# Forgetting and query columns as pairs among the mixer's first products, their sums kept in PSUM, the recurrence projected first

## The chip, the cores and the metric

The kernel runs on one core of a Trainium2 chip. The time is device time in microseconds (us) of one execution of the whole block, from the first instruction to the last. Work is spread over the core's engines: TensorE (PE in the profile, its weight loads PEld), VectorE (DVE), ScalarE (ACT), GpSimd (POOL) and SyncE (SP), which here only issues transfers. Each engine runs its own list of instructions in a fixed order and waits at semaphores for what the others produce.

## What is computed

One layer of a decoder for 1024 positions of 1024 channels: a half-step SwiGLU feed-forward part (called ffn1 below), a token mixer, a second feed-forward part (ffn2), a last norm. Every matrix product is of 1024 x 1024 activations with a weight. The mixer, cut to what matters:

```python
q, f, i, og, u, ga, gb = jnp.split(h @ w_in, IN_SPLITS, axis=-1)
q = silu(q) * DK ** -0.5
fg = lb + (1.0 - lb) * jax.nn.sigmoid(f)          # forgetting
o = hgrn2_chunked(q, 1 - fg, i, log(fg))          # 8 heads, gated linear recurrence
o = o * lax.rsqrt(mean(o * o) + EPS) * hgrn_g * silu(og)
y_a = o @ hgrn_w_o
ua, ub = jnp.split(u, 2, axis=-1)
u = causal_depthwise_conv(ua * sigmoid(ub), conv_w, conv_b)    # 31 taps
y_b = silu(layer_norm(u, conv_ln_g, conv_ln_b)) @ conv_w_o
return (sigmoid(ga) * y_a + sigmoid(gb) * y_b) @ w_out
```

q, f, i, og, ga and gb are 8 columns of 128 channels each, u is 16.

## The kernel before

Activations lie with channels on the 128 partitions and positions along the row, in two halves of 512 positions. Every fp32 matrix product is made of three fp32r products, high x high, high x low and low x high; `split` makes the two parts, the high one with a cast on ACT (L90) and the low one with a subtraction on DVE (L91). One matrix instruction multiplies a 128x128 weight tile with a 128x512 operand and adds into one PSUM bank. A column (128 outputs, 8 weight tiles, two halves) made directly takes 8 x 2 x 3 = 48 of them (`mm3`, L104 to L106), a pair of columns 96.

`paired` makes a pair of columns with seven products instead of eight quarter products, each of 4 x 3 = 12 instructions (`mmw`, L232 to L234), so 84 in all. For that it needs sums of quarter operands. The right operands' sums (x11, x12, x21, x22 of the activations, 16 for a stage) are subtractions on POOL, L290, once per stage; their splits are the tiles `hq`, `bq` and some of `h`. The weights' sums (four for a pair, L251 and L306) and splits (seven) are on DVE and ACT, in `prepare`, one pair ahead. The products' sums (seven for a pair, L323 to L335) are on DVE and read PSUM; one copy out of PSUM, L321, is on ACT. The first two pairs of a stage are made directly (`warm`), while the norm of the stage before ends. `paired` runs three times: in ffn1, in the mixer and in ffn2.

The stages in order, with the stretch of the trace: ffn1 (0 to 697 us); the mixer's first products (697 to 1017), 16 pairs, namely 8 of u's columns (i and 8 + i, for the convolution) and 8 of the two gates' columns; the units (1017 to 1585); the merge (1585 to about 1850); ffn2. There are 8 units, one for each head of the recurrence. A unit makes four columns directly: forgetting, query, i and og, 192 instructions; then `head` makes the recurrence: six levels of decayed scores (L563, L579 on PE, then on DVE qa L583, k L584 and a masked copy out of PSUM L590), the states st (L618, L627), a norm (`on` L643 to L649, a reciprocal root of small DVE operations, L174 to L179), transposes on PE (L653) and the output og (L655). The depthwise convolution of one column (`conv`) is 1 + 30 DVE operations over 1024 positions (L541, L543); two of the eight (CONV_EARLY) run beside the mixer's first products, six in the units. At the end of the units stands the convolution's projection of the first half (`convolved(0)`). The merge projects the recurrence of each half, then mixes.

A scheduler lays the instructions out: it goes by priorities, which follow the order in which the code is written; a convolution is put back by `conv_delay`, so that its operations fill what DVE has free. Each engine then runs its list in that fixed order. POOL also holds some low splits of the warm pairs (L91 on POOL).

Of the kernel before, what the change touches and what calls it, by code (L numbers as in the profile page):

```python
# [8 lines left out]
F32 = mybir.dt.float32  # L9
# [19 lines left out]
CONV_EARLY = (1, 4)  # L29
# [11 lines left out]
class Block:  # L41
# [187 lines left out]
    def mmw(self, ps, w, i, x, first, last):  # L229
        wh, wl = w[:, 0, i * P:(i + 1) * P], w[:, 1, i * P:(i + 1) * P]  # L230
        mm = self.nc.tensor.matmul
        mm(ps, wh, x[:, 0, :], start=first, stop=False)  # L232
        mm(ps, wh, x[:, 1, :], start=False, stop=False)  # L233
        mm(ps, wl, x[:, 0, :], start=False, stop=last)  # L234
# [7 lines left out]
    def paired(self, ctx, h, hctx, src, order, warm, emit, after, right, ready=()):  # L242
# [17 lines left out]
        self.part(ctx, wp=11, hq=8, bq=4)  # L260
# [24 lines left out]
        b11, b21, b22 = ([b1[hh, k0 + i] for i in range(4)] for hh, k0 in ((0, 0), (0, 4), (1, 4)))  # L285
        t1, t2, t3, t4 = [], [], [], []
        for i in range(4):
            x11, x12, x21, x22 = h[0][i], h[1][i], h[0][4 + i], h[1][4 + i]
            for o, x, y in ((x11, x12, x11), (x12, x22, x12), (x22, x22, x11), (x21, x21, x22)):
                nc.gpsimd.tensor_tensor(o, x, y, op=sub)  # L290
            t2.append(hq(x22))
            t3.append(hq(x12))
            t1.append(self.parts(x11))
            t4.append(self.parts(x21, self.bq, "bq"))
        hctx.close()
        self.part(ctx, right=True, **right)

        def product(ps, w, xs):
            for i in range(4):
                self.mmw(ps, w, i, xs[i], i == 0, i == 3)  # L300

        def prepare(f):
            ra, rb = load(f)
            a11, a12, a21, a22 = ra[:, :T], ra[:, T:], rb[:, :T], rb[:, T:]
            w11, w12, w22 = wop(a11), wop(a12), wop(a22)
            V.tensor_tensor(a22, a21, a22, op=add)  # L306
            tt(a21, a11, a21)
            tt(a11, a22, a11)
            tt(a12, a12, a11)
            ws2, ws3, ws1, ws4 = wop(a11), wop(a21), wop(a22), wop(a12)  # L310
            return w11, w12, w22, ws1, ws2, ws3, ws4

        ops = None
        for n, f in enumerate(order):
            if f not in fs:
                w11, w12, w22, ws1, ws2, ws3, ws4 = ops if ops else prepare(f)
                ops = prepare(order[n + 1]) if n + 1 < len(order) else None
                p1, p2, p3, p4, p5, p6, p7 = [self.acc() if (7 * n + i) % 2 == 0 else self.bank() for i in range(7)]
                product(p1, w11, b11)
                c11, c21, c22, u = (self.piece() for _ in range(4))  # L320
                A.copy(u, p1)  # L321
                product(p2, w12, b21)
                V.tensor_tensor(c11, p2, u, op=add)  # L323
                product(p3, ws2, t2)
                V.tensor_tensor(u, p3, u, op=add)
                product(p4, ws3, t3)
                V.tensor_tensor(c22, p4, u, op=add)
                product(p5, w22, t4)
                V.tensor_tensor(c21, p5, c22, op=add)
                emit(f, 0, c11, c21, c21)  # L330
                product(p6, ws1, t1)
                V.tensor_tensor(c22, p6, c22, op=add)
                V.tensor_tensor(u, p6, u, op=add)
                product(p7, ws4, b22)
                V.tensor_tensor(u, p7, u, op=add)  # L335
                emit(f, 1, u, c22, c22)
            after(n, f)
# [6 lines left out]
    def ffn(self, h, hctx, w_in, w_out, gate, warm, residual, norm, done, between=None):  # L344
# [6 lines left out]
        gs = {f: [] for f in order}  # L351
# [4 lines left out]
        def swiglu(f, hh, a, b, dst):  # L356
            s = self.half()
            if dst is None:
                dst = self.half()
            A.activation(s, a, AF.Silu)  # L360
            V.tensor_tensor(dst, b, s, op=ALU.mult)
            gs[f].append(dst)

        def combos(i):

            (x11, x12), (x21, x22) = gs[i], gs[NKK + i]
# [135 lines left out]
    def role(self, tag, shape=(P, S), bufs=2):  # L502
        pool = self.up if tag in ("u", "fg", "k", "q", "og", "v") else self.vp
# [11 lines left out]
    def unit(self, c, hs):  # L515
# [14 lines left out]
        for i, evac in ((8, ev_f), (0, self.silu_into(q)), (16, ev_i), (24, self.silu_into(og))):  # L530
            self.column(hs, self.weight(w_in[i + c]), evac)
# [21 lines left out]
    def head(self, c, fg, k, v, q, og):  # L553
# [96 lines left out]
        for b in range(2):  # L650
# [4 lines left out]
            V.scalar_tensor_tensor(og[:, sl], ps, self.col(C_HG, c), og[:, sl], op0=ALU.mult, op1=ALU.mult)  # L655
            nc.sync.dma_start(self.o_dram[b][c], og[:, sl])
# [20 lines left out]
    def run(self):  # L677
# [4 lines left out]
        self.o_dram = [[self.dp.tile([P, T], F32, name=f"od{h}{i}") for i in range(8)] for h in range(2)]  # L682
# [3 lines left out]
        self.u_dram = [[self.dp.tile([P, T], F32, name=f"ad{h}{i}") for i in range(8)] for h in range(2)]  # L686
        self.z_dram = [[self.dp.tile([P, T], F32, name=f"zd{h}{i}") for i in range(8)] for h in range(2)]
# [103 lines left out]
        def mix_in(f, hh, x, y, dst):  # L791
            sx = x if dst is not None else self.half()
            A.activation(sx, x, AF.Sigmoid)
            if f >= NH:
                sy = y if dst is not None else self.half()
# [3 lines left out]
            elif f in CONV_EARLY:  # L799
                if hh == 0:  # L800
# [11 lines left out]
        with ExitStack() as ctx:  # L812
            w_mix = lambda f, b: a["mix_w_in"][(40 - 8 * b + f) if f < NH else (48 + 8 * b + f - NH)]
            b1 = self.paired(ctx, xs, hctx, w_mix, [f for i in range(NH) for f in (i, NH + i)], warm, mix_in, after,
                             dict(cq=8, up=1, vp=1), ready)
# [3 lines left out]
        late = [c for c in range(NH) if c not in CONV_EARLY]  # L819
        with ExitStack() as ctx:  # L820
            self.part(ctx, wp=8, mp=1, up=2, vp=2, ln=8)
# [16 lines left out]
            for c in range(NH):  # L838
                if c < len(late):
                    u = self.role("u", bufs=1)  # L840
                    for h in range(2):
                        nc.sync.dma_start(u[:, h * T:(h + 1) * T], self.u_dram[h][late[c]])
                    self.conv(late[c], u)
                if c == NH - 1:
                    xc = self.layer_norm(0)
                self.unit(c, h2)
            self.convolved(0, xc)
# [3 lines left out]
        with ExitStack() as inner:  # L851
            self.part(inner, wp=8, gt=4, ol=8, ln=8, nq=3)
# [62 lines left out]
    def merge(self):
# [106 lines left out]
```

## Time and profile before

| | us |
|---|---|
| median of 3 runs | 2467.28 |
| lowest and highest | 2462.15, 2468.10 |
| the profiled execution, its own time | 2467.12 |
| its span in the trace | 2465.3 |
| PE busy in it | 2405.5 |
| DVE busy in it | 2010.2 |
| ACT busy in it | 944.8 |
| POOL busy in it | 116.9 |

The span is what the trace covers; the time has some 1.8 us around it. Busy time is the union of an engine's instructions; those of an engine overlap a little (the next one starts before the last one's end is drawn), so the distance from start to start of two like instructions is what one costs, and less than the duration given for it.

### The profile page before, as it was taken

Reading aid. Unit: us, or ns where it says so; the run is one execution under the profiler, and the core shown is the slowest. Engines: PE = TensorE matmul, PEld = TensorE weight load, DVE = VectorE, ACT = ScalarE, POOL = GpSimd, SP = SyncE. Lnnn points to the kernel's source line nnn. Section 1 sums busy time; section 2 is a strip of 40 time slices with the busy share of each in tenths; the row PEclk is TensorE's granted clock in tenths of the full one; section 3 lists DMA queues with packets and bytes.
Section 4 is the critical chain, followed back from the end, with each engine's and each line's share of the span. In section 5 each row is a group of like instructions: output and inputs, shape, how many; then the busy total and the mean of one; then the engine's idle time right before and its main releaser. Section 6 shows DMA issues by size and latency. Waiting matters only on the chain.

```text
span 2465.3 us, 30875 instructions
## 1 busy us (share of the span) xinstructions
PE 2405.5 (98%) x11320; PEld 1992.7 (81%) x11320; DVE 2010.2 (82%) x3010; ACT 944.8 (38%) x1679; POOL 116.9 (5%) x77
## 2 busy tenths in 40 slices
PE   4999999999999999999999999999999999999997
PEld 3788887888878888788888888888888888888886
DVE  8999999778889999799999877575568777775977
ACT  4522223344644333233333335453343333324443
POOL 3300000000050000000000000000050000000000
PEclk9999999999999999999999999999999999999998
DMA  7156665595523323311212112774523233228743
GB/s 277 68 190 208 202 203 186 174 344 176 171 86 116 106 83 104 105 52 65 68 44 65 56 56 90 241 251 162 159 80 124 86 107 117 93 86 298 269 128 124
DMA packets 139975, 346.46 MB, mean 141 GB/s; under 512 B 15536, under 2 KB 15664, under 8 KB 139824
## 3 DMA queue, kind: packets, MB, share of 16 engines
q1 hardware_dynamic: 139680, 343.97, 41.7%
q8 instruction: 89, 1.46, 0.2%
q10 hardware_dynamic: 144, 0.52, 0.1%
q14 instruction: 62, 0.51, 0.1%
HBM read 266.31 MB, written 78.12 MB: 140 GB/s over the span
## 4 chain that ended last, share of the span: by engine, by line
PE 80%; DVE 12%; DMA 5%; issue 2%; ACT 1%; POOL 0%; SPq 0%; DVEq 0%; ACTq 0%
PE pa L233 8%; PE pa L234 8%; PE pa L232 8%; PE pb L232 8%; PE pb L234 8%; PE pb L233 8%; PE pa L106 8%; PE pa L104 8%; PE pa L105 8%; PE pb L579 3%; DMA ada<-in_ada_w_dram 2%; DVE w L91 2%; DMA ra<-in_ffn_w_in_dram 1%; DVE ada L154 1%; DVE ra L251 1%
## 5 line engine op out<-in xcount | busy, mean ns | idle before, releaser
L90 ACT CAST w<-ra 128x512 fp32r<-128x512 f32 x402 | 238.4, 619 | 436.5 <-DMA ra<-in_ffn_w_in_dram 110.8
L104 PE MATMUL pa<-h,wh 128*128 128x512 f32 x896 | 355.4, 397 | 1.5 <-ACT wh L90 1.5
L106 PE MATMUL pa<-h,wl 128*128 128x512 f32 x896 | 353.7, 395 | 1.8 <-DVE wl L91 1.8
L105 PE MATMUL pa<-h,wh 128*128 128x512 f32 x896 | 353.3, 394 | 0.0
L543 DVE SCALAR_TENSOR_TENSOR uc<-u,par,uc 128x1023 f32<-128x1023 f32 (+14 forms) x240 | 303.1, 1263 | 2.7
L91 DVE TENSOR_TENSOR w<-ra,w 128x512 fp32r<-128x512 f32 x378 | 254.8, 690 | 10.0 <-ACT w L90 9.4
L232 PE MATMUL pa<-h,w 128*128 128x512 f32 x504 | 199.3, 398 | 5.8 <-ACT h L90 4.1
L233 PE MATMUL pa<-h,w 128*128 128x512 f32 x504 | 199.7, 396 | 2.9 <-DVE h L91 2.9
L234 PE MATMUL pb<-h,w 128*128 128x512 f32 x504 | 197.4, 392 | 4.1 <-POOL w L91 4.0
L234 PE MATMUL pa<-h,w 128*128 128x512 f32 x504 | 198.1, 393 | 0.0
L106 PEld LDWEIGHTS pa<-h,wl 128*128 128x128 f32 x896 | 168.6, 188 | 36.0 <-DVE wl L91 2.5
L104 PEld LDWEIGHTS pa<-h,wh 128*128 128x128 f32 x896 | 168.8, 188 | 35.3 <-ACT wh L90 2.3
L233 PE MATMUL pb<-h,w 128*128 128x512 f32 x504 | 197.0, 391 | 0.0
L232 PE MATMUL pb<-h,w 128*128 128x512 f32 x504 | 196.7, 391 | 0.0
L105 PEld LDWEIGHTS pa<-h,wh 128*128 128x128 f32 x896 | 168.9, 189 | 33.2 <-issue 0.7
L90 ACT CAST ob<-br 128x512 fp32r<-128x512 f32 x154 | 95.8, 622 | 198.6 <-PE pb L234 80.1
L90 ACT CAST wh<-raw 128x1024 fp32r<-128x1024 f32 x80 | 84.0, 1051 | 205.5 <-PE pa L105 192.6
L91 DVE TENSOR_TENSOR ob<-br,ob 128x512 fp32r<-128x512 f32 x154 | 106.7, 694 | 67.5 <-ACT ob L90 66.8
L233 PE MATMUL pa<-ob,oa 128*128 128x512 f32 x352 | 137.5, 391 | 1.5 <-DVE ob L91 1.5
L232 PE MATMUL pa<-ob,oa 128*128 128x512 f32 x352 | 137.1, 390 | 0.0
L234 PE MATMUL pa<-ob,oa 128*128 128x512 f32 x352 | 137.0, 389 | 0.0
L360 ACT ACTIVATE s<-c 128x512 f32<-128x512 f32 x80 | 50.6, 633 | 185.4 <-DVE c L335 127.6
(233 smaller groups left out, 5015.6 us busy)
## 6 DMA issues: line engine op xcount, KB each, us to landing
ra<-in_ffn_w_in_dram SPq DMA_DIRECT2D x88, 512.0 KB, 4.2
br<-bd SPq DMA_DIRECT2D x154, 256.0 KB, 3.2
bd<-c SPq DMA_DIRECT2D x146, 256.0 KB, 2.0
ada<-in_ada_w_dram SPq DMA_DIRECT2D x72, 512.0 KB, 4.4
ar<-in_ffn_w_out_dram SPq DMA_DIRECT2D x88, 256.0 KB, 4.5
ra<-in_mix_w_in_dram SPq DMA_DIRECT2D x32, 512.0 KB, 3.8
raw<-in_mix_w_in_dram SPq DMA_DIRECT2D x32, 512.0 KB, 3.5
ar<-in_ffn_w_out_dram SPq DMA_DIRECT2D x22, 512.0 KB, 4.8
```

The lines of the kernel that those rows point to most:

```text
L90: self.nc.scalar.copy(hi, src)
L91: (eng or self.nc.vector).tensor_tensor(lo, src, hi.bitcast(F32), op=ALU.subtract)
L104: mm(ps, wh, x[:, 0, :], start=first, stop=False)
L105: mm(ps, wh, x[:, 1, :], start=False, stop=False)
L106: mm(ps, wl, x[:, 0, :], start=False, stop=last)
L154: self.nc.vector.scalar_tensor_tensor(raw, raw, 1.0, self.cs, op0=ALU.mult, op1=ALU.mult, accum_out=dst)
L232: mm(ps, wh, x[:, 0, :], start=first, stop=False)
L233: mm(ps, wh, x[:, 1, :], start=False, stop=False)
L234: mm(ps, wl, x[:, 0, :], start=False, stop=last)
L360: A.activation(s, a, AF.Silu)
L543: V.scalar_tensor_tensor(uc[:, j:], u[:, :S - j], cw(KC - 1 - j), uc[:, j:], op0=ALU.mult, op1=ALU.add)
L579: mm(ps[0:n, i * 64:(i + 1) * 64], ch(k, i)[:, 0:n], two(ch(qa, i))[:, :, 1, :], start=True, stop=True)
```

## The change

- Forgetting and query columns, eight pairs, go from the units into the mixer's `paired`. Two of the eight gate pairs (GATES_LATE) go out of it and become direct columns at the end of the units. The mixer's `paired` then has 22 pairs, two of them warm. The results are stored to memory (f_dram, q_dram) and loaded by the unit, where Sigmoid and Silu read them from there.
- In the mixer's `paired` (`inbank=True`) sums of products are made by PE in PSUM: `chain` takes w11 b11, is copied by ACT (p1), goes on with ws2 t2, is copied (u2), goes on with ws3 t3 and at last w22 t4; `low` takes ws1 t1, is copied (p6), goes on with ws4 b22. DVE keeps three sums for a pair (seven before), ACT has three copies (one before). The last two products of a pair run among the next pair's.
- The right operands' sums of all three `paired` go from POOL to DVE, with the first `prepare` ahead of them.
- Four convolutions run early, four in the units, at every second one.
- o of the first half stays on chip; the recurrence of both halves is projected first in the merge, with the layer norm of the first half inside it, and `convolved(0)` follows there.

```diff
-CONV_EARLY = (1, 4)
+CONV_EARLY = (1, 2, 4, 5)
+GATES_LATE = (6, 7)
...
+    def sooner(self, n):
+        return self.defer(-n)
...
-        self.part(ctx, wp=11, hq=8, bq=4)
+        self.part(ctx, wp=9 if inbank else 11, **({"w22": 2} if inbank else {}), hq=8, bq=4)
...
-        for i in range(4):
-            x11, x12, x21, x22 = h[0][i], h[1][i], h[0][4 + i], h[1][4 + i]
-            for o, x, y in ((x11, x12, x11), (x12, x22, x12), (x22, x22, x11), (x21, x21, x22)):
-                nc.gpsimd.tensor_tensor(o, x, y, op=sub)
...
+        ops = prepare(order[2])
...
+        for x11, x12, x21, x22 in xx:
+            tt(x11, x12, x11)
+        if inbank:
+            part1()
+        for x11, x12, x21, x22 in xx:
+            tt(x12, x22, x12)
+            tt(x22, x22, x11)
+            t2.append(hq(x22))
+            t3.append(hq(x12))
+        for x11, x12, x21, x22 in xx:
+            tt(x21, x21, x22)
+            t4.append(self.parts(x21, self.bq, "bq"))
...
+        def up(dst, src):
+            with self.sooner(200):
+                A.copy(dst, src)
+        def third(chain, ws3, t3, p6, c12, c22, f):
+            product(chain, ws3, t3, True)
+            with self.sooner(200):
+                V.tensor_tensor(c22, chain, p6, op=add)
+            emit(f, 1, c12, c22, c22)
+        def fourth(chain, w22, c11, n, f):
+            product(chain, w22, t4, True)
+            emit(f, 0, c11, chain, c11)
+            after(n, f)
...
+            product(chain, w11, b11)
+            up(p1, chain)
+            if not old:
+                second()
+            if old:
+                third(*old[0])
+            product(low, ws1, t1)
+            up(p6, low)
+            if old and not last:
+                second()
+            product(chain, ws2, t2, True)
+            up(u2, chain)
+            if old:
+                fourth(*old[1])
+            product(low, ws4, b22, True)
+            V.tensor_tensor(c12, low, u2, op=add)
...
-        for i, evac in ((8, ev_f), (0, self.silu_into(q)), (16, ev_i), (24, self.silu_into(og))):
+        for h in range(2):
+            sl = slice(h * T, (h + 1) * T)
+            nc.sync.dma_start(fg[:, sl], self.f_dram[h][c])
+            nc.sync.dma_start(q[:, sl], self.q_dram[h][c])
+        for h in range(2):
+            sl = slice(h * T, (h + 1) * T)
+            ev_f(fg[:, sl], h, sl)
+            A.activation(q[:, sl], q[:, sl], AF.Silu)
+        for i, evac in ((16, ev_i), (24, self.silu_into(og))):
...
-                if c < len(late):
-                    u = self.role("u", bufs=1)
+                if c % 2 == 0:
+                    u = self.role("u")
...
-            self.convolved(0, xc)
+            for c in GATES_LATE:
+                for b in range(2):
...
+                    self.column(h2, self.weight(a["mix_w_in"][48 + 8 * b + c]), ev_g)
```

How the lists of instructions change. First PE in the fourth unit, from the transposes that end its head (L653 before, L754 after). In the names, `pa` and `pb` are PSUM banks, `wh` and `wl` the high and low parts of a column's weight, `on` the normed recurrence, `q` and `k` the next head's. Before, the transposes, with columns (L104 to L106) behind them:

```order
L106 MATMUL pa_12014<-h_5439,wl_12011 128x512
L653 MATMUL pb_11841<-par,on_11798 128x128 x2
L104 MATMUL pa_12014<-h_5442,wh_12010 128x512
L653 MATMUL pb_11848<-par,on_11798 128x128 x2
L892 MATMUL pb_11855<-usum,mean 128x512
L653 MATMUL pb_11848<-par,on_11798 128x128 x2
L105 MATMUL pa_12014<-h_5442,wh_12010 128x512
```

After, where L110 to L112 are the columns, L664 and L680 the next head's scores:

```order
L754 MATMUL pb_11121<-par,on_11078 128x128 x2
L111 MATMUL pa_11627<-h_6216,wh_11597 128x512
L754 MATMUL pb_11128<-par,on_11078 128x128
L664 MATMUL pb_11268<-q_11137,k_11136 128x128
L754 MATMUL pb_11128<-par,on_11078 128x128 x2
L664 MATMUL pb_11268<-q_11137,k_11136 128x128
L754 MATMUL pb_11128<-par,on_11078 128x128
L664 MATMUL pb_11268<-q_11137,k_11136 128x128 x2
L664 MATMUL pb_11274<-q_11137,k_11136 128x128 x4
L680 MATMUL pb_11283<-qa_11280,k_11136 128x64 x8
L112 MATMUL pa_11627<-h_6216,wl_11598 128x512
```

Between a head's transposes and the next head's first scores 50 to 94 column instructions stood before; now the next head begins among the transposes. From head to head there are 192 column instructions before, and 118, 115, 122, 110, 110, 97 and 100 after.

Second, DVE in the middle of one mixer pair. `c` tiles are the products' sums, `ra` a weight's quarter and its sums, `w` a low split, `uc` the convolution. Before:

```order
L323 TENSOR_TENSOR c_1283_7493<-pa_1277_7475,c_1286_7496 128x512
L543 SCALAR_TENSOR_TENSOR uc_1266_7410<-u_1265_7379,par_81,uc_1266_7410 128x1022
L325 TENSOR_TENSOR c_1286_7496<-pb_1278_7476,c_1286_7496 128x512
L91 TENSOR_TENSOR w_1275_7471<-ra_1267_7445,w_1275_7471 128x512
L543 SCALAR_TENSOR_TENSOR uc_1266_7410<-u_1265_7379,par_81,uc_1266_7410 128x1021
L327 TENSOR_TENSOR c_1285_7495<-pa_1279_7477,c_1286_7496 128x512
L91 TENSOR_TENSOR w_1289_7589<-ra_1287_7585,w_1289_7589 128x512
L543 SCALAR_TENSOR_TENSOR uc_1266_7410<-u_1265_7379,par_81,uc_1266_7410 128x1020
L329 TENSOR_TENSOR c_1284_7494<-pb_1280_7478,c_1285_7495 128x512
```

After:

```order
L425 TENSOR_TENSOR c_1291_7579<-pb_1286_7574,c_1290_7578 128x512
L260 TENSOR_TENSOR ra_1277_7546<-ra_1276_7544,ra_1277_7546 128x512
L97 TENSOR_TENSOR w_1280_7555<-ra_1277_7546,w_1280_7555 128x512
L97 TENSOR_TENSOR w_1281_7558<-ra_1276_7544,w_1281_7558 128x512
L260 TENSOR_TENSOR ra_1276_7544<-ra_1277_7546,ra_1276_7544 128x512
L644 SCALAR_TENSOR_TENSOR uc_1237_7225<-u_1235_7169,par_81,uc_1237_7225 128x1006
L97 TENSOR_TENSOR w_1282_7563<-ra_1276_7544,w_1282_7563 128x512
L385 TENSOR_TENSOR c_1292_7580<-pa_1285_7573,c_1288_7576 128x512
```

The sums that read PSUM come further apart; L385, L408 and L425 are the three that are left.

Third, the right operands' sums at the start of ffn1's products. On POOL before:

```order
L290 TENSOR_TENSOR x_312<-x_316,x_312 128x512
L290 TENSOR_TENSOR x_315<-x_317,x_315 128x512
L290 TENSOR_TENSOR x_317<-x_317,x_311 128x512
L290 TENSOR_TENSOR x_313<-x_313,x_317 128x512
L290 TENSOR_TENSOR x_315<-x_317,x_315 128x512
```

On DVE after, where s (L454) is the warm pairs' output and hq a split:

```order
L97 TENSOR_TENSOR w_874<-ra_848,w_874 128x512
L260 TENSOR_TENSOR x_336<-x_340,x_336 128x512 x2
L260 TENSOR_TENSOR x_339<-x_341,x_339 128x512 x2
L260 TENSOR_TENSOR x_341<-x_341,x_335 128x512 x2
L260 TENSOR_TENSOR x_340<-x_342,x_340 128x512 x2
L454 TENSOR_TENSOR s_833<-pa_491,s_832 128x512
L454 TENSOR_TENSOR s_837<-pb_579,s_836 128x512
L97 TENSOR_TENSOR hq_883<-x_341,hq_883 128x512
```

They stand on DVE behind the first pair's weight splits and ahead of the splits of their own results. In all PE has 10582 matrix instructions before and 10510 after; the 72 fewer are all of 128x512 (504 more for six more pairs in the mixer, 768 fewer for two columns in each of eight units, 192 more for the late gates).

## Rows read from the trace of the kernel before

**Rows 1.** The page's busy time of each engine: us, share of the span, instructions.
```profile
PE 2405.5 (98%) x11320; PEld 1992.7 (81%) x11320; DVE 2010.2 (82%) x3010; ACT 944.8 (38%) x1679; POOL 116.9 (5%) x77
```
**Rows 2.** Busy time by stretch, us: start, ffn1's and mixer's products, units, merge.
```profile
core 0: us, PE busy (x) PEld busy (x) DVE busy (x) ACT busy (x) POOL busy (x), PEclk, DMA share, GB/s
0.00:100.00 100.00, 63.56 (x221) 46.46 (x222) 88.04 (x155) 51.19 (x87) 41.63 (x28) 0.95 0.44 171
100.00:420.00 320.00, 317.85 (x1394) 260.70 (x1394) 293.52 (x492) 95.45 (x170) 0.00 (x0) 1.00 0.60 196
697.00:1017.00 320.00, 315.87 (x1381) 260.60 (x1379) 284.22 (x385) 118.97 (x202) 29.57 (x19) 0.99 0.29 99
1017.00:1585.00 568.00, 566.65 (x3303) 484.93 (x3302) 481.87 (x641) 212.55 (x448) 0.00 (x0) 1.00 0.24 77
1585.00:1850.00 265.00, 263.74 (x1166) 216.32 (x1165) 175.28 (x239) 113.56 (x165) 36.23 (x24) 1.00 0.52 173
```
**Rows 3.** Timeline of PE in a dense stretch: start, duration, engine, line, operation.
```profile
684.77 0.39 PE L234 MATMUL pa<-ob,oa 128*128 128x512 f32 x1
...
686.81 0.39 PE L234 MATMUL pa<-ob,oa 128*128 128x512 f32 x1
```
**Rows 4.** Timeline from the mixer's last product to the first unit: PE, then ACT.
```profile
1014.50 0.39 PE L234 MATMUL pb<-h,w 128*128 128x512 f32 x1
1016.06 0.50 PE L104 MATMUL pa<-h,wh 128*128 128x512 f32 x1 [1.18 <-ACT wh L90]
...
1016.86 0.40 PE L105 MATMUL pa<-h,wh 128*128 128x512 f32 x1
1017.53 0.49 PE L104 MATMUL pa<-h,wh 128*128 128x512 f32 x1 [0.27 <-ACT wh L90]
1018.61 0.50 PE L106 MATMUL pa<-h,wl 128*128 128x512 f32 x1 [0.58 <-DVE wl L91]
...
1014.97 1.04 ACT L90 CAST wh<-raw 128x1024 fp32r<-128x1024 f32 x1 [1.15 <-PE pb L234]
```
**Rows 5.** Busy time in two whole units, the second cut at its head's end, and another head.
```profile
1126.40:1191.50 65.10, 65.09 (x390) 56.16 (x389) 60.54 (x77) 22.22 (x51) 0.00 (x0) 1.00 0.19 62
...
1191.50:1256.70 65.20, 65.17 (x390) 56.11 (x389) 60.72 (x78) 23.67 (x52) 0.00 (x0) 1.00 0.20 65
1191.50:1239.80 48.30, 48.27 (x316) 42.12 (x314) 44.17 (x64) 20.86 (x47) 0.00 (x0) 1.00 0.20 66
1239.80:1256.70 16.90, 16.90 (x77) 13.99 (x77) 16.55 (x15) 2.81 (x5) 0.00 (x0) 1.00 0.19 63
1256.70:1304.90 48.20, 48.19 (x316) 42.33 (x315) 43.49 (x64) 20.60 (x47) 0.00 (x0) 1.00 0.17 52
```
**Rows 6.** The page's groups: line, engine, tiles, count, busy us, mean ns.
```profile
L543 DVE SCALAR_TENSOR_TENSOR uc<-u,par,uc 128x1023 f32<-128x1023 f32 (+14 forms) x240 | 303.1, 1263 | 2.7
```
**Rows 7.** Groups of the units by shape, DVE.
```profile
L91 DVE TENSOR_TENSOR wl<-raw,wh 128x1024 fp32r<-128x1024 f32 x40 | 48.8, 1222 | 9.8 <-ACT wh L90 8.1 <-PE pa L106 1.5
L583 DVE TENSOR_TENSOR qa<-qa,ff 128x512 f32<-128x512 f32 x48 | 33.2, 691 | 28.4 <-PE pb L579 27.3
L590 DVE COPY_PREDICATED att<-msk,pb 128x512 f32<-128x512 uint8 x32 | 32.0, 1001 | 0.0
```
**Rows 8.** Groups of the mixer's products by shape, DVE and ACT.
```profile
L91 DVE TENSOR_TENSOR w<-ra,w 128x512 fp32r<-128x512 f32 x98 | 65.9, 693 | 2.6 <-ACT w L90 2.4
L251 DVE TENSOR_TENSOR ra<-ra,ra 128x512 f32<-128x512 f32 x28 | 19.2, 686 | 0.3
L91 DVE TENSOR_TENSOR hq<-x,hq 128x512 fp32r<-128x512 f32 x8 | 10.6, 1365 | 0.0
L335 DVE TENSOR_TENSOR c<-pa,c 128x512 f32<-128x512 f32 x7 | 4.8, 691 | 3.1 <-PE pa L234 2.8
...
L321 ACT COPY c<-pa 128x512 f32<-128x512 f32 x7 | 4.1, 587 | 7.2 <-PE pa L234 7.2
```
**Rows 9.** Groups of the whole kernel on POOL.
```profile
L290 POOL TENSOR_TENSOR x<-x,x 128x512 f32<-128x512 f32 x48 | 79.8, 1683 | 55.2 <-ACT x L216 37.9 <-issue 6.6 <-DVE h L91 3.9
```
**Rows 10.** The tile hq at ffn1: DVE's splits, PE's first uses; starts, first to last.
```profile
L91 DVE TENSOR_TENSOR hq<-x,hq x8: 672/677/1786, 77.5 to 94.7; 128x512 fp32r<-128x512 f32 x8
...
L232 PE MATMUL pa<-hq,w x8: 389/389/397, 103.5 to 127.6; 128*128 128x512 f32 x8
```
**Rows 11.** The waits: who waited for what, us in all, times, longest.
```profile
DVE qa L583 <- PE pb L579: 29.0, 40, 2.4
```
**Rows 12.** The page's DMA issues: tiles, queue, count, KB each, median us to landing.
```profile
br<-bd SPq DMA_DIRECT2D x154, 256.0 KB, 3.2
bd<-c SPq DMA_DIRECT2D x146, 256.0 KB, 2.0
```

More of the change, by code (lines that the diff above doesn't have):

```diff
@@ L227, in parts, with mmw, paired @@
         return t
-    def mmw(self, ps, w, i, x, first, last):
+    def mmw(self, ps, w, i, x, first, last, more=False):
         wh, wl = w[:, 0, i * P:(i + 1) * P], w[:, 1, i * P:(i + 1) * P]
+        kw = {"skip_group_check": True} if more else {}
         mm = self.nc.tensor.matmul
[L232 to L242, printed above, removed]
+        mm(ps, wh, x[:, 0, :], start=first, stop=False, **kw)
+        mm(ps, wh, x[:, 1, :], start=False, stop=False, **kw)
+        mm(ps, wl, x[:, 0, :], start=False, stop=last, **kw)
+    def paired(self, ctx, h, hctx, src, order, warm, emit, after, right, ready=(), inbank=False):
         nc = self.nc
@@ L304, in prepare @@
             a11, a12, a21, a22 = ra[:, :T], ra[:, T:], rb[:, :T], rb[:, T:]
[L305 to L310, printed above, removed]
-            return w11, w12, w22, ws1, ws2, ws3, ws4
-        ops = None
-        for n, f in enumerate(order):
[L315 to L337, printed above, removed]
@@ new lines, in up, with second @@
+        def up(dst, src):
[9 more added lines that the diff above has]
+            emit(f, 0, c11, chain, c11)
+            after(n, f)
+        old = None
+        for n, f in enumerate(order):
+            if f in fs:
+                after(n, f)
+                continue
+            last = n + 1 == len(order)
+            w11, w12, w22, ws1, ws2, ws3, ws4 = ops
+            if not last:
+                ops = prepare(order[n + 1])
+            chain, low = self.acc(), self.bank()
+            p1, p6, c11, u2, c12, c22 = (self.piece() for _ in range(6))
+            def second():
+                left = self.bank()
+                product(left, w12, b21)
+                V.tensor_tensor(c11, left, p1, op=add)
+            product(chain, w11, b11)
[14 more added lines that the diff above has]
+            V.tensor_tensor(c12, low, u2, op=add)
+            old = (chain, ws3, t3, p6, c12, c22, f), (chain, w22, c11, n, f)
+            if last:
+                third(*old[0])
+                second()
+                fourth(*old[1])
@@ L350, in ffn @@
         order = [f for i in range(NKK) for f in (i, NKK + i)]
-        gs = {f: [] for f in order}
+        gs = {f: {} for f in order}
         def tt(dst, a, b):
@@ L791, in mix_in @@
         def mix_in(f, hh, x, y, dst):
+            if f >= 2 * NH:
+                for s, to in ((x, self.f_dram), (y, self.q_dram)):
+                    if s is not x and not hh:
+                        s = self.piece()
+                        A.copy(s, y)
+                    nc.sync.dma_start(to[hh][f - 2 * NH], s)
+                return
             sx = x if dst is not None else self.half()
@@ L794, in mix_in @@
             if f >= NH:
-                sy = y if dst is not None else self.half()
+                sy = y if dst is not None and hh else self.half()
                 A.activation(sy, y, AF.Sigmoid)
@@ L799, in mix_in @@
             elif f in CONV_EARLY:
-                if hh == 0:
+                if f not in us:
                     us[f] = self.role("u")
```

151 lines of the change are left out of this document (105 added, 46 removed).

## The prediction

> **What bounds the kernel now.** I read the page's busy times first. PE is busy for 98% of the span, DVE for 82%, ACT for 38% [rows 1]. The same by stretch shows that no stage is an exception: PE has 317.85 us of 320 in ffn1's products, 315.87 of 320 in the mixer's, 566.65 of 568 in the units, 263.74 of 265 in the merge, and DVE is second everywhere, with 481.87 us in the units [rows 2]. So the time is a count of matrix instructions, and a change gains what it takes from PE's list as long as nobody makes PE wait. What one costs stands in a dense stretch of the timeline: ten like instructions, of which the first and the last are shown, start between 684.77 and 686.81 us, so 2.04 / 9 = 0.2267 us each; the 0.39 us beside them is a latency, since each starts before the last one is drawn as ended [rows 3]. The reader should then look where DVE is nearest to its limit. A unit takes 65.10 us, PE busy for 65.09 and DVE for 60.54, which is 93% [rows 5]. Within a unit the head has 44.17 us of DVE in 48.30 us (91%), the columns behind it 16.55 in 16.90 (98%).
>
> **The matrix instructions.** Six more pairs at 84 are 504 more, two columns of 48 in each of eight units 768 fewer, four late columns 192 more: 72 fewer, all of 128x512. 72 x 0.2267 = 16.3 us off PE. This is the one term that needs no assumption but that the places where they leave from and go to are both dense, and both are [rows 2].
>
> **From the mixer to the units.** Three starts are late there: 1014.50 to 1016.06, 1016.86 to 1017.53 and 1017.53 to 1018.61 us, which is 1.56 + 0.67 + 1.08 less three times 0.23, so 2.6 us. ACT's first cast of a unit's weight stood 1.15 us waiting for the mixer's last product [rows 4], because the weight's tile takes memory that this product still reads. After the change that last product reads a low-numbered pool of its own (w22), and the tiles of the others are let go a product earlier or more. The stall may go (2.6) or stay (0), since the late wl split of DVE is a second cause that is still there. Nothing says which it is nearer to; I take half, 1.3.
>
> **The mixer's own products.** The stage grows to 22 pairs. DVE's work in it: 284.2 us now [rows 2]; 42 splits and 24 sums of weights more at under 0.69 each (+46), 35 sums of products fewer at 0.691 (-24), 16 sums of right operands (+11) [rows 8], two convolutions brought forward, of which 45 operations lie ahead of the first head by the lists (45 x 1.263 = 57 [rows 6]). That is 374 us in a stage of 320 + 504 x 0.2267 = 434 us, 86% after 89% now: DVE gets no tighter. ACT gets 42 casts and 54 copies of 0.59 each [rows 8], 57 us more on 119, 41% of the stage. I cost both at nothing, because PE covers them; where the cover would fail is the second rival. The 32 stores and 32 loads of forgetting and query are of a kind that lands in 2.0 and 3.2 us [rows 12], issued a pair or a unit ahead on SP's queue, and they take the place of nothing that PE waits for: nothing too.
>
> **Sums in PSUM.** A new wait arises: PE may go on adding into `chain` or `low` only when ACT has copied what is there. The nearest row is the copy that exists, 0.587 us [rows 8]. By PE's list 36 instructions of other products stand between a product and the next one into the same bank, 36 x 0.2267 = 8.2 us, and the same between the third product, which DVE's sum L425 reads, and the fourth. So the price is 0 unless ACT or DVE is over 7.6 us late, and 20 pairs x 3 copies x 0.587 = 35 us if the cover were gone. I take 0. The Trainium skill ("PSUM — Partial Sum Buffer", section "PSUM bank collisions raise a hardware error") says that TensorE must not write a bank while ScalarE reads it, so the wait for every copy is a real one and speaks against sums in PSUM; if nothing stood between, it would make the sum 35 us worse, and with the 8.2 us it changes nothing. No run so far shows a read between two products of one bank.
>
> **The right operands' sums.** POOL needs 1.683 us for one [rows 9], DVE 0.686 for the like of it [rows 8]; 16 at each of three starts are 11 us on DVE. But DVE pays for POOL's today: the splits of hq, which run beside them, take 1.365 us where the like split of w takes 0.693 [rows 8], (1.365 - 0.693) x 8 = 5.4 us for these alone, and other splits run there too. Does PE feel either? In ffn1 hq's last split starts at 94.7 us and PE's first use of hq at 103.5 [rows 10], so 8.8 us cover. At worst, with nothing given back, 11 - 8.8 = 2.2 us late at each start, 6.6 in all; at best the warm stretch of ffn1, where DVE is the bound (88.04 us of 100 [rows 2]), ends 2 us earlier, an estimate from the 5.4. I take 0.
>
> **The units.** This is where the change is tight. A unit goes from 192 columns' instructions to 118, 115, 122, 110, 110, 97, 100, on average 110, so PE needs 65.1 - 82 x 0.2267 = 46.6 us for it. DVE loses less in proportion. In the lists a unit with a whole convolution in it has 26 of its operations, after 13 to 17, on average 15.6; wl splits go from 4.5 to 2.3, and half a sum of 1.2 us goes: 10.4 x 1.263 + 2.2 x 1.222 + 0.6 = 16.4 us [rows 6, 7]. 60.6 - 16.4 = 44.2 us [rows 5], 95% of 46.6, where it was 93%; in the units with 97 and 100 columns PE needs 43.6 and 44.2, and DVE is level with it. Today 98% is reached only where PE makes columns and DVE convolves [rows 5], and that stretch goes: the next head starts among the transposes. On the other side DVE's 9% of idleness in a head is not a limit of DVE. It waits for PE, 29.0 us in 40 levels, 0.7 each, since PE puts columns between the scores [rows 11]; with 8 to 10 columns in a level in place of 9 to 11 it waits less, and works when it would have waited. So the price lies between 0 and that of the first rival (12 us). I take 3, nearer to the lower end, for the two units that are level.
>
> **The merge.** The same products in another order, at 263.74 us of 265 [rows 2]: 0, at most the 1.3 us that are idle off, or as much more.
>
> **The sum.** Against the profiled execution, 2467.1 us (median 2467.3, so the same): 2467.1 - 16.3 - 1.3 + 0 + 0 + 3 = 2452.5 us.
>
> **Rivals.** *DVE keeps its 91% in heads.* If what a head allows is 44.17 in 48.30, then a unit that is all head needs 44.2 / 0.914 = 48.4 us, 1.8 more than PE, and seven of them 12.6 in place of my 3: 2462 us. For it: the head behind shows the same, 43.49 in 48.20 us [rows 5]. Against: the waits just told, which have PE as their releaser. It decides as soon as DVE can't pass 95%.
>
> *The copies out of PSUM are late* (the other side). ACT's list is in order. If a copy stands behind a Sigmoid that waits for DVE's sum, and DVE is behind with convolutions, then PE stands before the next product into that bank. At one copy's length each that is 35 us: 2452.5 + 35 = 2487 us. It decides from 7.6 us of lateness on. Against: DVE at 86% and ACT at 41% in the stage, and the copies are put ahead in ACT's list by 200 of the scheduler's steps.
>
> *The sums at the starts show in full*: 6.6 us, 2459 us, still faster by little. *The gain isn't there at all* would need the 72 instructions to have lain in idle time of PE; it has 60 us of that in the whole span [rows 1], 36 of them in the first 100 us [rows 2], so this has no chance worth a number.
>
> **How the numbers follow.** By more or less than 0.3% (7.4 us) is about what a measurement of this kernel tells from no change, so the bounds are 2459.9 and 2474.7. My forecast, with the sums at the starts, 0.76; the first rival, inside the bounds, 0.16; the copies 0.08. Faster 0.76, same 0.16, slower 0.08. The range: at the low end the transition's 2.6, ffn1's 2, the units' 0 and the merge's 1.3, 2467.1 - 16.3 - 2.6 - 2 - 1.3 = 2445; at the high end the first rival and the sums at one or two starts, 2462 + 4 = 2466. The copies are left out.
>
> **What would show it.** Right: 0.2267 us from start to start in the mixer's products with no gap at the chain's products, units some 46 to 47 us apart, DVE at 94 to 96% in them, waits of DVE for qa shorter than 0.7. Wrong: PE waiting in the scores or the states for DVE's qa, k or st, units of 48 us and more (first rival); PE waiting for ACT's c in the mixer (second); gaps of PE at hq or the first chain after a warm stretch (third). The sum falls if the units' DVE work is more than 46 us, because no term but the 16.3 us is large enough to make up for it.

## The result and the profile after

| | before, us | after, us |
|---|---|---|
| median | 2465.51 (4 runs) | 2445.26 (4 runs) |
| lowest to highest | 2462.15 to 2468.10 | 2441.72 to 2447.96 |
| profiled execution, its span | 2465.3 | 2441.7 |

The ratio is 0.9918, with a 95% interval of 0.9898 to 0.9938: faster by 0.8%, 20 us, where 14.8 were forecast. 2445.3 lies at the very low end of the range (2445 to 2466). So more was gained than the sum explains, and the question is where.

The page's busy times of after, in the form of [rows 1]:

```profile
span 2441.7 us, 30694 instructions
PE 2382.8 (98%) x11248; PEld 1976.7 (81%) x11248; DVE 1986.2 (81%) x3066; ACT 984.2 (40%) x1763; POOL 37.4 (2%) x29
```

PE has 72 instructions fewer, as counted, and it is still busy for 98%. Busy time by stretch, in the form of [rows 2]: the start, ffn1's products, the mixer's products, the units and the merge of after.

```profile
0.00:100.00 100.00, 69.33 (x262) 51.65 (x263) 88.18 (x177) 56.98 (x96) 14.04 (x12) 1.00 0.49 189
100.00:420.00 320.00, 320.00 (x1414) 264.96 (x1413) 304.43 (x514) 98.73 (x174) 0.00 (x0) 1.00 0.59 198
697.00:1117.00 420.00, 419.16 (x1848) 346.39 (x1846) 365.00 (x477) 162.09 (x284) 0.96 (x1) 1.00 0.29 100
1117.00:1513.00 396.00, 391.77 (x2529) 341.66 (x2530) 350.13 (x509) 184.98 (x417) 0.00 (x0) 1.00 0.22 73
1513.00:1790.00 277.00, 273.99 (x1210) 223.91 (x1208) 168.69 (x247) 112.15 (x157) 6.92 (x6) 1.00 0.59 190
```

PE makes 262 instructions in the first 100 us where it made 221 [rows 2], the granted clock is 1.00 there and was 0.95, and ffn1's products have lost their last idle time. To see what each stretch gave, I took the start of the same instruction in both traces. "Matrix work" is the number of instructions between two marks that went or came, times 0.2267 us.

| mark | before | after | gained in this stretch | of it matrix work |
|---|---|---|---|---|
| ffn1: first hq product | 103.45 | 94.21 | 9.2 | 0 |
| ffn1: last output product | 696.31 | 683.42 | 3.7 | 0 |
| units: first column | 1016.06 | 1117.78 | -114.6 | -114.3 (504) |
| merge: last column | 1809.73 | 1783.41 | 128.0 | 130.6 (576) |
| ffn2: first output product | 2236.17 | 2213.64 | -3.8 | 0 |
| ffn2: last output product | 2448.00 | 2424.85 | 0.6 | 0 |
| PE's last instruction | 2455.73 | 2431.76 | 0.8 | 0 |

In all 24.0 us in these two traces: 16.3 of matrix work, 12.9 in ffn1 and 1.4 in ffn2's last products, less 3.8 at ffn2's start, 2.6 in the units and the merge and 0.3 in the mixer. (The two traced executions lie 23.6 us apart and the medians 20.3, so some 3 us of the table belong to these executions.) ffn1's 12.9 us were not in the sum.

What made them shows first on DVE. First the kernel before: the busy times by stretch of 40 to 100 us, and rows of DVE's and POOL's timelines (start, duration, engine, line; in brackets how long the engine was idle before, and who ended that).

```profile
40.00:100.00 60.00, 51.33 (x193) 39.29 (x194) 59.93 (x86) 31.76 (x54) 35.35 (x20) 0.91 0.08 27
...
57.74 2.28 POOL L290 TENSOR_TENSOR x<-x,x 128x512 f32<-128x512 f32 x1 [3.29 <-DVE mod L163]
...
58.80 1.77 DVE L91 TENSOR_TENSOR bq<-x,bq 128x512 fp32r<-128x512 f32 x1
...
63.40 1.46 POOL L290 TENSOR_TENSOR x<-x,x 128x512 f32<-128x512 f32 x1 [3.38 <-issue]
...
63.63 1.25 DVE L159 TENSOR_TENSOR mod<-mod,par 128x1 f32<-128x1 f32 x1
```

The same of after:

```profile
40.00:100.00 60.00, 57.02 (x234) 44.40 (x234) 59.96 (x108) 37.46 (x63) 7.84 (x4) 1.00 0.16 57
...
56.59 0.68 DVE L97 TENSOR_TENSOR bq<-x,bq 128x512 fp32r<-128x512 f32 x1
...
60.32 0.15 DVE L165 TENSOR_TENSOR mod<-mod,par 128x1 f32<-128x1 f32 x1
```

DVE counts as busy for all of the 60 us in both, but it does 86 instructions before and 108 after. A split that takes 0.68 us alone takes 1.77 beside a sum of POOL; an operation on one element of each partition (mod) takes 1.25 where it takes 0.15, so it is a wait of 1.1 us and not slow work. POOL waits in its turn: the sum at 57.74 takes 2.28 us, the one at 63.40 1.46. The Trainium skill ("SBUF — State Buffer", section "Who interferes with whom") says that a DVE instruction with two inputs in SBUF and a GpSimd instruction that reads SBUF exclude each other for a whole instruction; these rows agree, with up to 1.1 us as the price of a meeting for DVE.

How this reaches PE is seen from who ends PE's waits. PE has the same 236 instructions ahead of ffn1's first hq product in both kernels; its waits between 40 us and there add up to 8.6 us before and 2.9 after. The two longest of before, from PE's timeline, and one row of ACT's:

```profile
52.82 0.79 PE L234 MATMUL pb<-h,w 128*128 128x512 f32 x1 [4.02 <-POOL w L91]
...
70.59 0.73 PE L232 MATMUL pa<-h,w 128*128 128x512 f32 x2 [2.40 <-ACT h L90]
...
68.17 0.62 ACT L90 CAST hq<-x 128x512 fp32r<-128x512 f32 x1 [2.68 <-POOL x L290]
```

The 4.02 us are a wait for a low split of POOL itself, which stands behind a sum on POOL's own list. The 2.40 us are a wait for casts of ACT, which had stood 2.68 us for one of POOL's sums. Only 1.5 of the 8.6 us, in three waits, are ended by splits of DVE. So POOL's work holds up PE in three ways, through DVE, through ACT and directly; no run separates them, since an instruction that is moved from POOL to DVE takes all three away at once. Some 3.5 of the 9.2 us are not waits. An estimate from these rows puts them to the clock: in 50 to 60 and 70 to 80 us of before, behind these two waits, the granted clock fell to 0.66 and 0.83:

```profile
50.00:60.00 10.00, 7.18 (x22) 5.72 (x23) 10.00 (x16) 2.59 (x4) 6.71 (x4) 0.66 0.29 91
...
70.00:80.00 10.00, 7.50 (x24) 4.90 (x24) 10.00 (x15) 4.99 (x10) 7.98 (x5) 0.83 0.00 0
```

where after, whose longest wait there is 1.06 us, has 1.00 in the same stretches. The loss at ffn2 shows the same meeting with POOL's other work, the low splits of the warm pairs' weights: PE waits once for such a split and once for DVE's scalings. Rows of PE's, DVE's and POOL's timelines of after:

```profile
1786.94 0.73 PE L242 MATMUL pa<-h,w 128*128 128x512 f32 x2 [1.34 <-POOL w L97]
...
1794.44 1.12 PE L204 MATMUL pb<-s,ones 128*128 128x512 f32 x2 [1.72 <-DVE s L202]
...
1786.93 1.74 DVE L217 TENSOR_TENSOR s<-s,s 128x512 f32<-128x512 f32 x1 [2.34 <-ACT s L216]
...
1791.55 2.83 DVE L202 TENSOR_SCALAR s<-par,t 128x128 f32<-128x128 f32 x4
...
1784.37 6.69 POOL L97 TENSOR_TENSOR w<-ra,w 128x512 fp32r<-128x512 f32 x5 [2.67 <-ACT w L96]
```

The norm's square sum s, 0.69 us in the kernel before, takes 1.74 while POOL splits, and the four scalings take 2.83 us in place of 0.87.

### The profile page after: what moved, and what is told of

Its sections match the earlier page's. It is cut to its first block, busy times and chain, and to the rows that moved or that the text cites. A ratio compares the mean times of both kernels' runs of the same rounds, so it can differ in the third digit from the quotient of the medians.

```text
span 2441.7 us, 30694 instructions
## 1 busy us (share of the span) xinstructions
PE 2382.8 (98%) x11248; PEld 1976.7 (81%) x11248; DVE 1986.2 (81%) x3066; ACT 984.2 (40%) x1763; POOL 37.4 (2%) x29
## 4 chain that ended last, share of the span: by engine, by line
PE 92%; DVE 4%; ACT 2%; DMA 1%; issue 1%; POOL 0%; DVEq 0%; SPq 0%; POOLq 0%; ACTq 0%
PE pa L241 12%; PE pa L242 12%; PE pa L240 12%; PE pb L242 10%; PE pb L241 10%; PE pb L240 10%; PE pa L111 6%; PE pa L112 6%; PE pa L110 6%; PE pb L680 3%; PE pb L704 1%; DVE s L217 1%; PE pb L739 1%; DVE ada L160 1%; PE pb L719 1%; PE pb L664 1%
## 5 line engine op out<-in xcount | busy, mean ns | idle before, releaser
L96 ACT CAST w<-ra 128x512 fp32r<-128x512 f32 x444 | 261.5, 620 | 391.3 <-PE pa L242 114.9
L97 DVE TENSOR_TENSOR w<-ra,w 128x512 fp32r<-128x512 f32 x420 | 278.9, 689 | 34.2 <-ACT w L96 33.6
L110 PE MATMUL pa<-h,wh 128*128 128x512 f32 x704 | 280.6, 399 | 2.6 <-ACT wh L96 2.6
L112 PE MATMUL pa<-h,wl 128*128 128x512 f32 x704 | 279.1, 397 | 0.5 <-DVE wl L97 0.5
L111 PE MATMUL pa<-h,wh 128*128 128x512 f32 x704 | 279.2, 397 | 0.0
L242 PE MATMUL pb<-h,w 128*128 128x512 f32 x632 | 246.0, 389 | 1.1 <-POOL w L97 1.1
L241 PE MATMUL pb<-h,w 128*128 128x512 f32 x632 | 245.9, 389 | 0.0
L240 PE MATMUL pb<-h,w 128*128 128x512 f32 x632 | 245.4, 389 | 0.0
L240 PE MATMUL pa<-h,w 128*128 128x512 f32 x472 | 186.6, 398 | 2.8 <-ACT h L96 2.8
L241 PE MATMUL pa<-h,w 128*128 128x512 f32 x472 | 186.1, 394 | 1.6 <-DVE h L97 1.5
L242 PE MATMUL pa<-h,w 128*128 128x512 f32 x472 | 185.2, 393 | 1.3 <-POOL w L97 1.3
L110 PEld LDWEIGHTS pa<-h,wh 128*128 128x128 f32 x704 | 132.8, 189 | 30.2 <-ACT wh L96 4.1
L112 PEld LDWEIGHTS pa<-h,wl 128*128 128x128 f32 x704 | 132.7, 189 | 26.4 <-DVE wl L97 1.0
L111 PEld LDWEIGHTS pa<-h,wh 128*128 128x128 f32 x704 | 132.7, 189 | 25.8 <-issue 0.7
L242 PEld LDWEIGHTS pb<-h,w 128*128 128x128 f32 x632 | 118.6, 188 | 26.1 <-POOL w L97 1.5
L240 PEld LDWEIGHTS pb<-h,w 128*128 128x128 f32 x632 | 118.6, 188 | 24.7
L241 PEld LDWEIGHTS pb<-h,w 128*128 128x128 f32 x632 | 118.6, 188 | 24.6
L241 PE MATMUL pa<-ob,oa 128*128 128x512 f32 x352 | 137.3, 390 | 1.3 <-DVE ob L97 1.3
```

The costliest lines, as they stand in the source:

```text
L96: self.nc.scalar.copy(hi, src)
L97: (eng or self.nc.vector).tensor_tensor(lo, src, hi.bitcast(F32), op=ALU.subtract)
L240: mm(ps, wh, x[:, 0, :], start=first, stop=False, **kw)
L241: mm(ps, wh, x[:, 1, :], start=False, stop=False, **kw)
L242: mm(ps, wl, x[:, 0, :], start=False, stop=last, **kw)
```

## The experiments

Theory 1: POOL's instructions hold up DVE's (and, as said above, ACT and PE), and taking the sums away from POOL is what gains in ffn1. Theory 2: the new order gains, with the first pair's weight splits ahead of the sums. Four kernels tell them apart.

**Only the engine.** The kernel before with

```diff
-                nc.gpsimd.tensor_tensor(o, x, y, op=sub)
+                V.tensor_tensor(o, x, y, op=sub)
```

> The kernel before, with the right operands' sums on DVE at their old place in the code, nothing else. Theory 1 (POOL's sums hold up DVE's splits while they run): PE reaches the first hq product of ffn1 about 9 us earlier than 103.5 us, ffn1 ends about 13 us earlier than 696.3, ffn2's start loses about 4, in all some 9 us under the kernel before, 2456. Theory 2 (it is the new order, the first weights' splits ahead of the sums, that gains): within 3 us of the kernel before, since DVE gets 11 us of work at each start and nothing else changes.

Measured 2460.64 us against 2464.11 (ratio 0.9985, 0.9975 to 0.9994): 3.5 gained, not 9. In its trace ffn1's last output product starts 6.2 us earlier than before, half of the 12.9. The warm stretch is better, but then PE stands once, by its timeline:

```profile
93.68 0.80 PE L234 MATMUL pa<-h,w 128*128 128x512 f32 x1 [3.95 <-DVE w L91]
```

and DVE's timeline shows what that split of a weight stood behind:

```profile
91.74 0.68 DVE L91 TENSOR_TENSOR h<-x,h 128x512 fp32r<-128x512 f32 x1
92.34 0.68 DVE L290 TENSOR_TENSOR x<-x,x 128x512 f32<-128x512 f32 x1
92.94 0.68 DVE L91 TENSOR_TENSOR w<-ra,w 128x512 fp32r<-128x512 f32 x1
```

Sums and splits of the right operands now stand ahead of the first pair's weight.

**Only the order.** The kernel before with the first `prepare` ahead and the sums by kind, on POOL.

```diff
+        ops = prepare(order[2])
...
+        for x11, x12, x21, x22 in xx:
+            nc.gpsimd.tensor_tensor(x11, x12, x11, op=sub)
...
```

> The kernel before, with the sums still on POOL, but in the changed kernel's order: the first prepare ahead, sums by kind, then splits. Theory 1: no gain, 2465, the hq product of ffn1 at 103 us. Theory 2: 9 us gained, 2456, the hq product near 94 us.

2464.25 us (ratio 0.9996, 0.9986 to 1.0005): nothing, as theory 1 has it. Its 40 to 100 us look like those of the kernel before, 85 instructions of DVE:

```profile
40.00:100.00 60.00, 47.98 (x185) 36.91 (x184) 60.00 (x85) 34.08 (x60) 34.22 (x20) 0.91 0.13 44
```

**Both, and none of the pairs.** The edit above, with the sums on DVE.

> The kernel before with both, order and DVE: the whole of this part of the change without the pairs. Both theories: 13 us gained in ffn1, 4 lost at ffn2, some 9 us under the kernel before, 2456. If the rest of the change is what gains in ffn1, nothing.

2452.66 us (ratio 0.9950, 0.9935 to 0.9965): 11.5 gained. ffn1's last output product starts 14.0 us earlier than before. The two parts gain 6.2 and 1.5 apart and 14.0 together: the engine frees DVE, and the order keeps what DVE took over from standing in PE's way. ffn2's start loses only 0.1 here, so the expected loss of 4 was wrong in this kernel.

**The changed kernel with the sums on POOL.**

```diff
-            tt(x11, x12, x11)
+            nc.gpsimd.tensor_tensor(x11, x12, x11, op=sub)
...
```

> The changed kernel with the sums back on POOL, its order kept. Theory 1: the gain of ffn1 goes (+13) and ffn2's loss too (-4), some 9 us over the changed kernel, 2454. Theory 2: as the changed kernel, 2445.

2456.47 us (ratio to before 0.9964, 0.9951 to 0.9977), 11 over the changed kernel's median, 12.6 if each is compared with the kernel before that was measured beside it. The first hq product of ffn1 starts at 104.24 us again. But ffn2's start still loses 3.9 us between the merge's last column and the first output product. So that loss isn't of the sums on DVE; it comes with the new merge, behind which the last norm and POOL's low splits fall together (it isn't in the third kernel, which has the splits and the old merge).

**POOL emptied.** If POOL is what costs, its 24 remaining splits should cost as well.

```diff
-            ws[f] = [[self.parts(r[:, i * T:(i + 1) * T], self.wp, "w", nc.gpsimd) for i in range(2)] for r in load(f)]
+            ws[f] = [[self.parts(r[:, i * T:(i + 1) * T], self.wp, "w") for i in range(2)] for r in load(f)]
```

> The changed kernel with the last work of POOL, the low splits of the warm pairs' weights (24 of 128x512), on DVE too. If POOL's reads are what holds DVE up, the stall of PE at the start of ffn2 (1.5 + 1.9 us around 1785 to 1794, where DVE's s takes 1.74 and 2.83 us beside POOL's splits) goes, and ffn1's warm stretch ends 2 us earlier: 5 us under the changed kernel, 2440. If DVE has no room for the splits (8 x 0.6 = 5 us at each start), no gain, or up to 5 us slower.

2433.93 us (ratio 0.9878, 0.9863 to 0.9893): 11 under the changed kernel's median, 9.5 if each is compared with the kernel before measured beside it: about twice what was expected, and the fastest version here. Against the changed kernel's trace 2.1 us come from ffn1's warm stretch, 1.3 before ffn1 ends, 5.0 from the mixer's start, 2.3 from ffn2's. So 2.3 of the 3.8 us lost at ffn2 are POOL's; 1.5 stay without it. DVE's scalings behind the last norm, on its timeline, in place of the rows of 1786.93 and 1791.55 above:

```profile
1779.28 0.69 DVE L217 TENSOR_TENSOR s<-s,s 128x512 f32<-128x512 f32 x1
...
1782.44 0.29 DVE L202 TENSOR_SCALAR s<-par,t 128x128 f32<-128x128 f32 x1
...
1783.84 0.68 DVE L202 TENSOR_SCALAR s<-par,t 128x128 f32<-128x128 f32 x3
```

**What is left for the pairs.** The kernel before with order, sums and splits on DVE, so that POOL is as empty as in the last one.

> The kernel before with the sums on DVE, the first prepare ahead of them, and the warm pairs' low splits on DVE too: POOL empty in both this and e5, so the difference between the two is the pairs, the sums in PSUM and the merge's order alone. e3 without the splits gave 2452.7. If the splits gain here what they gained in the changed kernel without its ffn2 stall (2.1 in ffn1, some 5 around the mixer's start), 2445 to 2446, and the pairs are worth 11 to 12 of the 16.3 us that their 72 instructions cost. If the gain of e5 came wholly from the changed kernel's own places, 2452.

2445.85 us (ratio 0.9923, 0.9906 to 0.9939), as fast as the whole change, without its pairs. Against the version with POOL emptied, 2433.93, the pairs with all that belongs to them are worth some 11 to 12 us (11.9 by the medians, 10.6 by what each gains over the kernel before measured beside it) of the 16.3 that their instructions cost.

**The sums in PSUM.** The changed kernel with `inbank` off in the mixer (a copy on ACT that only `inbank` needs is left out too). The mixer then also prepares its weights, lays out its buffers and orders its products as in the kernel before.

```diff
-                             dict(cq=8, cu=1), ready, inbank=True)
+                             dict(cq=8, cu=1), ready)
```

> The changed kernel with the mixer's products summed on DVE as before (seven sums for a pair) and not in PSUM, the 22 pairs kept. DVE gets 4 x 20 x 0.6 = 48 us more in a stage of 434 us, 86 to 97%. If that is over what DVE can give there, PE waits: 10 to 30 us slower, 2455 to 2475. If the sums in PSUM bought nothing, the same time, 2445.

2470.78 us (ratio to before 1.0026, 1.0016 to 1.0036): 26 over the changed kernel, slower even than the kernel before. As a number that is what was expected, but not at the place: the mixer's products are dense, with DVE busy for 390.79 us of 410:

```profile
720.00:1130.00 410.00, 408.93 (x1804) 338.32 (x1804) 390.79 (x524) 125.74 (x208) 0.96 (x1) 1.00 0.31 104
```

and the unit's first column starts within 2 us of the changed kernel's. The price comes later. Rows of PE's and DVE's timelines at the first head:

```profile
1154.90 2.08 PE L664 MATMUL pb<-q,k 128*128 128x128 f32 x8 [8.85 <-ACT k L618]
...
1140.11 5.97 DVE L644 SCALAR_TENSOR_TENSOR uc<-u,par,uc 128x1016 f32<-128x1016 f32 x5
1146.00 1.22 DVE L649 TENSOR_TENSOR usum<-usum,uc 128x1024 f32<-128x1024 f32 x1
1147.14 6.50 DVE L644 SCALAR_TENSOR_TENSOR uc<-u,par,uc 128x1013 f32<-128x1013 f32 x5
1153.55 0.54 DVE L617 TENSOR_SCALAR fg<-fg,omlb,lb 128x512 f32<-128x512 f32 x1
```

The first head waits for k, which ACT makes from fg, and fg stands on DVE behind ten operations of the convolution. Against the changed kernel 17 us are lost before the first head starts, 4 in the units and 7 in the merge. Not all of it is waiting. In the units, behind these waits, a part of PE's time is at the lower of its two clock levels (1.2 and 2.4 GHz); here this run's units, then the changed kernel's:

```profile
1154.90:1527.23 372.33, 365.09 (x2376) 319.82 (x2377) 319.09 (x477) 172.04 (x395) 0.00 (x0) 0.97 0.18 57
...
1139.81:1508.37 368.56, 365.12 (x2415) 319.93 (x2414) 325.98 (x479) 160.37 (x387) 0.00 (x0) 1.00 0.20 62
```

So DVE's convolutions are a debt that moves to the next stage, and with the sums in PSUM it is smaller. In this arrangement the pairs gain only with them; how much of the 26 us is of the sums and how much of the rest that `inbank` changes was not taken apart.

**The copies out of PSUM.**

```diff
                 A.copy(dst, src)
+                A.copy(dst, src)
```

> The changed kernel with each copy of ACT out of PSUM made twice, 60 copies more of 0.59 us. If the 8.2 us of other products between a copy and the next product into its bank cover it, no change, within 1 us of 2445. If PE waits for copies, up to 60 x 0.5 = 30 us slower, 2475.

2443.14 us (ratio to before 0.9917, 0.9902 to 0.9931): as the changed kernel. A second copy takes 0.59 of the 7.6 us of cover, so this shows that the copies themselves are free, not how late one might come. The groups of ACT in its mixer show the second copies, 0.587 us each, and PE is busy for the whole of its 393 us there:

```profile
L381 ACT COPY c<-pa 128x512 f32<-128x512 f32 x40 | 23.5, 587 | 1.2
L380 ACT COPY c<-pa 128x512 f32<-128x512 f32 x40 | 23.5, 586 | 54.6 <-PE pa L242 53.4 <-DMA ra<-in_mix_w_in_dram 1.0
...
720.00:1113.00 393.00, 393.00 (x1735) 325.50 (x1734) 341.37 (x440) 175.76 (x312) 0.96 (x1) 1.00 0.29 101
```

**The units.** The late convolutions with 15 of their 30 multiply-adds left out.

```diff
-        for j in range(1, KC):
+        for j in range(1, taps):
...
-                    self.conv(late[c // 2], u)
+                    self.conv(late[c // 2], u, 16)
```

> The changed kernel with 15 of the 30 multiply-adds of each late convolution left out (their taps are missing in the output), so that DVE has 60 x 1.2 = 72 us less in the units, 9 of 45 in each. If DVE is what makes PE wait in the units, their gaps (0.5 + 1.4 + 0.5 + 1.5 us from 1145 to 1427) go and the time falls by 3 to 4 us, 2441. If the gaps come from chains of waits between engines, the time stays within 1 us.

2443.31 us (ratio to before 0.9914, 0.9899 to 0.9929), 2 under the changed kernel's median, and 20.4 under the kernel before measured beside it, where the changed kernel has 20.3: no change. The changed kernel's gaps in the units are these, on PE's timeline:

```profile
1382.97 1.30 PE L680 MATMUL pb<-qa,k 128*128 128x64 f32 x10 [1.19 <-DVE k L685]
...
1428.21 0.97 PE L680 MATMUL pb<-qa,k 128*128 128x64 f32 x7 [1.48 <-DVE k L685]
...
1514.67 0.50 PE L110 MATMUL pa<-h,wh 128*128 128x512 f32 x1 [1.03 <-ACT wh L96]
```

With fewer taps the first two are gone, and in their place the gap behind the last head has grown:

```profile
1510.06 0.80 PE L110 MATMUL pa<-h,wh 128*128 128x512 f32 x1 [3.25 <-ACT wh L96]
```

So DVE's load, and the order that the scheduler makes of it, does cause the gaps within the units, but they are worth 3 us, and what is behind them takes them back: from the first unit column to the merge's last column the changed kernel is 665.6 us long and this one 665.9. A part of what is taken back is the clock, which was granted at 0.77 from 1505 to 1520 us, behind the wait of 3.25, and at 1.00 in the changed kernel. Which of load and order it is, this kernel doesn't tell, since the lists differ too.

## Why the prediction held, and where it didn't

- **The matrix instructions: right.** 72 fewer, 0.2267 us each. Where POOL is empty in both, the pairs gain some 11 to 12 of the 16.3 us.
- **From the mixer to the units: right.** The stall was 2.6 us [rows 4] and is one gap of 2.00 - 0.23 = 1.8, so 0.8 gained where 1.3 were put (the mixer's products lose 1.2 us elsewhere, so that the stretch as a whole is level).
- **The mixer's products and the sums in PSUM: right in the cost** (0). DVE was busy for 365.0 of 420 us there, 87%, where 86% were worked out (with 35 sums of products fewer, where the lists have 14 x 7 - 20 x 3 = 38; 2 us). PE was busy for 419.16 of these 420 us and copying twice costs nothing, so the late copies, the second rival, did not come. What I had not said is that the sums in PSUM are needed at all: without them, and what goes with them, the kernel is 7 us slower than the one before measured beside it. I costed DVE's work in the mixer at nothing, because PE covers it there; 48 us more of it cost 26 us in the units and the merge.
- **The right operands' sums: the step that failed.** I took 0, with 2 us at best. ffn1 gave 12.9. I had the row that shows it [rows 8, hq at 1365 ns] and priced eight splits of one tile, then asked whether PE feels the sums themselves [rows 10], and found 8.8 us of cover. But PE had been waiting, all through the warm stretch, for other work that POOL held up: for POOL's own split behind a sum (4.02 us), for ACT's casts behind a POOL sum (2.40), and for splits of DVE (1.5). The profile of before showed DVE with all of its time busy between 40 and 100 us and POOL working beside it; a timeline of DVE there, with its one-element operations of 1.25 us, would have shown that DVE was standing, and PE's rows who ended its waits. hq's first use itself moved by 9.2 us, so a cover measured to it was a cover to something late.
- **The units: right.** 3 us were put, and from the first column to the last of the merge 2.6 were lost. The heads of after start 45.2 to 49.0 us apart, 47.1 on average (1139.8 to 1469.8 us in seven steps), against 46.6. The load of DVE was put too high, 44.2 us to a unit; here a full window of seven units of after, in the form of [rows 5]:

```profile
1139.80:1469.80 330.00, 326.56 (x2142) 286.11 (x2141) 302.55 (x436) 144.69 (x342) 0.00 (x0) 0.99 0.20 62
```

  302.55 / 7 = 43.2 us, 92%. That is where the first rival put the limit of a head, but PE is busy for 326.56 of these 330 us, so DVE's idle time is mostly that of an engine that waits for a full one. Whether DVE could have gone beyond 92% there wasn't tried, and the rival's 12 us did not come.
- **Waits for qa: wrong in detail.** 32.0 us in 45 waits of DVE, 0.71 each, as long as before [rows 11], where I expected shorter ones.
- **ffn2's start: not seen.** I costed the merge at 0, as the same products in another order. The new order put the last norm beside POOL's low splits, and 3.8 us were lost; 2.3 of them came back when POOL was emptied, and what the other 1.5 are stays open.

The forecast had the sign and, just, the range. The sum's own error is mostly one term, what POOL's sums cost the other engines, put at 0 where ffn1 gave 12.9 us; ffn2's 3.8 us the other way made up for a part of it. That the time still fell inside the range, by 0.3 us, is luck.

## What to carry to other kernels

An engine that shows as busy all the time can be standing: count its instructions in the stretch, and look for the shortest operation that takes a microsecond. Then ask of each wait of PE who ended it: here the longest were ended by POOL and by ACT, not by DVE. Work on POOL is not free when DVE is near its limit; before a sum is put there to relieve DVE, compare the splits of DVE with and without POOL beside them. What is taken from an engine that is not the bound in its stage can still be worth what a deferred job of it, here a convolution, no longer pushes into the next stage.

## What the runs showed of the hardware

- A POOL subtraction of 128x512 (1.68 us on average) costs DVE up to 1.1 us when an instruction of DVE on SBUF alone meets it, be that one short or long (0.15 to 1.25, 0.68 to 1.77), and is itself longer for it (2.28 against 1.46). DVE's L215, one of whose inputs is in PSUM, keeps its 0.7 us beside POOL, by the timeline of the kernel before:

```profile
66.62 1.39 DVE L215 SCALAR_TENSOR_TENSOR x<-x,mod,pb 128x512 f32<-128x512 f32 x2
...
66.84 5.86 POOL L290 TENSOR_TENSOR x<-x,x 128x512 f32<-128x512 f32 x3 [1.98 <-DVE h L91]
```

- PE went on adding into a PSUM bank that ACT had read in between, 60 times over, without a gap, also when each copy was made twice.
- Behind PE's waits of 4.02 and 2.40 us in the warm stretch the granted clock fell (0.66 and 0.83 of its upper level, 2.4 GHz, as means of 10 us, which is time at 1.2 GHz); in the kernel after, with waits of at most 1.06 us there, it stayed at 1.00.
